# A gated hybrid decoder layer on one core: inputs laid out transposed in HBM, an opening in another order, a stacked bias table, and dilated values computed in token order

## The chip, the core and the metric

The kernel runs on one core of a Trainium2 chip. The metric is the device time of one execution in microseconds (us), the median of several runs. The engines are TensorE (PE in the rows; PEld is its loading of the stationary operand), VectorE (DVE), ScalarE (ACT), GpSimd (POOL) and SyncE (SP). SP and ACT each own a hardware DMA queue, POOL a software one.

## What is computed

One layer of a decoder over 512 tokens of width 1024, with three branches that read the same x:

```
proj = x @ w_in                       # q, k, v of 12 heads; zb; qc
A: for 3 groups (window, dilation) = (128,1), (512,4), (2048,16), 4 heads each:
     s = q k^T / 8 + bias[bucket(distance)]   # keys gathered by stride
     o = softmax(s) v                 # groups merged by their denominators
B: u, vg = split(gelu(zb));  ob = u * (tril(w_spatial) @ layer_norm(vg) + b_spatial)
C: oc = softmax(qc kc^T / 8) vc       # kc, vc = mem @ w_mem_kv, 256 memory rows
y = (sum over branches of sigmoid(x @ w_gate + b_gate) * (branch @ w_proj)) @ w_out
h = layer_norm(alpha * x + y)
out = layer_norm(alpha * h + (gelu(causal_conv3(h @ w_a)) * (h @ w_b)) @ w_ffn_down)
```

## The kernel before

All values are fp32. A large product is made of three TensorE matmuls on a type called fp32r: each operand is split into a high part (a copy to fp32r by ScalarE, `hi`) and a low part (the rest, by VectorE, `lo`), and `mm3` adds low x high, high x low and high x high. `split_of` splits an activation, `emit_split` (L133, L134) a unit of weights.

Weights stream in a fixed order. `add_load`, `cols2` and `kcols` list the loads and the units (1024 columns per partition) in each; three raw buffers hold loads, four buffers hold split units, and `unit()` takes the next one after it has split two units ahead:

```
wraw = ctx.enter_context(tc.tile_pool(name="wraw", bufs=3))
wspl = ctx.enter_context(tc.tile_pool(name="wspl", bufs=4))
AHEAD = 2
```

x must lie with its features on the partitions, since TensorE contracts over partitions. Before, x comes in token rows, and `turn_x` turns it by 32 TensorE transposes of 128x128 (tile `tx`), copies the result out of PSUM and splits it into `xTh` and `xTl`. The opening is written out by hand for TensorE, ScalarE and VectorE (`manual_schedule`): 11 matmuls on zeros (`idle`, L370), then the transposes, mixed with the first products (`first_mm`, L384) of the first two of twelve 128-column groups of q and k, each in two halves of 256 tokens (t0, t1) and two halves of the contraction. The other ten groups follow as `qk` (L220, j = 2 to 11, 24 matmuls each).

After group j = 4, `prep_small` turns a tile of small parameters (`par`), and multiplies the bias table `relb` (33 rows) with one-hot rows of the bucket of each distance (`bkt`, 33 x 384 for each head group) into `vec`. From there four transfers on POOL's queue build the biases: `vec` to HBM (`vecs`), a repeated copy (`shear`), and three skewed reads (`bias`). Behind them on the same queue comes the load of `ws`, the spatial weights, which `prep_spatial` turns by 8 transposes and masks on VectorE.

Then come the values: `v0` (two units, for dilation 1) and `v12` (four units, for the other two groups). Groups 4 and 16 read the tokens by stride 4, so the stationary operand of `v12` is read by `xr`, every fourth token of xT.

Next `zb_part` computes the gMLP's inputs while `fill()` runs pieces of attention between its matmuls. Then mem is turned by 16 transposes (`tm`), and qc, kc, vc, the gates, the output projection and the FFN follow.

Behind the opening the program's order on each engine is set by a scheduler that places instructions by its own estimate of when they are ready; each engine then executes strictly in that order.

## Time and profile before

| | |
|---|---|
| median of 3 runs | 819.17 us (818.08 to 819.25) |
| profiled execution | 819.34 us |
| its span, first to last instruction | 817.6 us |
| TensorE matmul busy | 807.9 us, 99% of the span |
| VectorE, ScalarE busy | 382.2 us, 282.6 us |
| granted TensorE clock, mean | 0.999 |

The span is what the trace covers; 1.74 us of the profiled time lie outside it. A busy TensorE says only that matmuls were in it, so the time is read from the chain of work that ended last and from the spacing of matmuls.

### The profile page before, as it was taken

What the parts mean: (1) busy time and instruction counts of PE and PEld (TensorE: products, weight loads), DVE (VectorE), ACT (ScalarE), POOL (GpSimd) and SP (SyncE); (2) the same over time, 40 slices, a digit from 0 to 9 for tenths busy, and PEclk for the clock granted to TensorE, in tenths of its full rate; (3) what the DMA queues carried; (4) which work ended last, traced back from release to release, by engine and by line L of the source; (5) the groups of instructions that cost most, each with busy time, mean ns of one, the idle gap of its engine ahead of it and who ended that gap; (6) DMA issues with size and microseconds to landing.
All of it is one profiled execution on the core that took longest, in us unless ns stands there. A gap on an engine that the chain in (4) does not pass through costs nothing.

```text
span 817.6 us, 9710 instructions
## 1 busy us (share of the span) xinstructions
PE 807.9 (99%) x4048; PEld 672.7 (82%) x4048; DVE 382.2 (47%) x591; ACT 282.6 (35%) x431; POOL 20.4 (2%) x32
## 2 busy tenths in 40 slices
PE   8999999999999999999999999999999999999996
PEld 7878997778877788888888988888888888888885
DVE  4433245835664343435857454544444445225056
ACT  4322246663365132233511243333333333224000
POOL 2001000100000000000000000000000000000000
PEclk9999999999999999999999999999999999999999
DMA  8455231123402223243840033333333323234002
GB/s 319 137 180 186 104 129 52 53 78 122 137 26 78 71 93 120 81 152 108 307 152 1 1 103 103 103 103 104 103 103 103 103 89 127 94 103 155 1 26 78
DMA packets 61772, 87.64 MB, mean 107 GB/s; under 512 B 2107, under 2 KB 49259, under 8 KB 61729
## 3 DMA queue, kind: packets, MB, share of 16 engines
q1 hardware_dynamic: 59264, 81.81, 29.6%
q0 software_dynamic: 1408, 4.17, 1.4%
q10 hardware_dynamic: 1056, 1.05, 0.4%
q8 instruction: 32, 0.52, 0.3%
q14 instruction: 12, 0.09, 0.0%
HBM read 84.89 MB, written 4.48 MB: 109 GB/s over the span
## 4 chain that ended last, share of the span: by engine, by line
PE 98%; DMA 1%; DVE 0%; issue 0%; DVEq 0%; SPq 0%
PE y L220 20%; PE gate L220 16%; PE pa L220 13%; PE pb L220 13%; PE qk L220 7%; PE zb L220 6%; PE proj L220 5%; PE v L220 4%; PE up L220 3%; PE oT L559 1%; PE qk L384 1%; PE sc L559 1%; PE qc L220 1%; PE pt L528 1%; PE vc L220 1%; PE kc L220 1%
## 5 line engine op out<-in xcount | busy, mean ns | idle before, releaser
L134 DVE TENSOR_TENSOR wl<-raw,wh 128x1024 fp32r<-128x1024 f32 (+1 forms) x128 | 153.9, 1206 | 175.3 <-ACT wh L133 165.4
L133 ACT ACTIVATE wh<-raw 128x1024 fp32r<-128x1024 f32 (+1 forms) x128 | 133.0, 1043 | 183.3 <-PE pb L220 47.2
L220 PE MATMUL y<-wh,h 128*128 128x512 f32 x256 | 79.0, 389 | 0.0
L220 PE MATMUL gate<-xTh,wl 128*128 128x512 f32 x192 | 76.7, 400 | 0.0
L220 PE MATMUL gate<-xTh,wh 128*128 128x512 f32 x192 | 75.0, 390 | 0.0
L220 PE MATMUL gate<-xTl,wh 128*128 128x512 f32 x192 | 74.9, 390 | 0.0
L220 PE MATMUL pa<-hTh,wl 128*128 128x512 f32 x160 | 62.3, 389 | 0.0
L220 PE MATMUL pa<-hTl,wh 128*128 128x512 f32 x160 | 62.3, 389 | 0.0
L220 PE MATMUL pa<-hTh,wh 128*128 128x512 f32 x160 | 62.2, 389 | 0.0
L220 PE MATMUL pb<-hTh,wl 128*128 128x512 f32 x160 | 62.2, 389 | 0.0
L220 PE MATMUL pb<-hTl,wh 128*128 128x512 f32 x160 | 62.2, 389 | 0.0
L220 PE MATMUL pb<-hTh,wh 128*128 128x512 f32 x160 | 62.2, 389 | 0.0
L220 PEld LDWEIGHTS y<-wh,h 128*128 128x128 f32 x256 | 48.0, 188 | 10.0
L220 PE MATMUL y<-wl,h 128*128 128x512 f32 x128 | 49.8, 389 | 0.0
L941 DVE SCALAR_TENSOR_TENSOR c<-pa,par,c 128x511 f32<-128x511 f32 x20 | 15.0, 751 | 65.8 <-ACT c L940 65.8
L220 PEld LDWEIGHTS gate<-xTh,wl 128*128 128x128 f32 x192 | 36.1, 188 | 8.7 <-issue 1.2
L220 PEld LDWEIGHTS gate<-xTh,wh 128*128 128x128 f32 x192 | 36.0, 188 | 7.7
L940 ACT ACTIVATE c<-pa,par 128x512 f32<-128x512 f32 x20 | 15.6, 781 | 76.1 <-PE pa L220 76.1
L220 PEld LDWEIGHTS gate<-xTl,wh 128*128 128x128 f32 x192 | 36.1, 188 | 7.0
L220 PEld LDWEIGHTS pa<-hTh,wh 128*128 128x128 f32 x160 | 30.0, 188 | 6.3
L220 PEld LDWEIGHTS pb<-hTh,wl 128*128 128x128 f32 x160 | 30.0, 188 | 6.3
L220 PEld LDWEIGHTS pa<-hTh,wl 128*128 128x128 f32 x160 | 30.1, 188 | 6.2
(223 smaller groups left out, 1485.8 us busy)
## 6 DMA issues: line engine op xcount, KB each, us to landing
raw<-in_w_ffn_up SPq DMA_DIRECT2D x22, 1024.0 KB, 4.9
raw<-in_w_in SPq DMA_DIRECT2D x13, 1024.0 KB, 5.1
raw<-in_w_gate SPq DMA_DIRECT2D x12, 1024.0 KB, 4.9
raw<-in_w_ffn_down SPq DMA_DIRECT2D x11, 1024.0 KB, 4.9
raw<-in_w_out SPq DMA_DIRECT2D x4, 1024.0 KB
shear<-vecs POOLq DMA_DIRECT2D x1, 2304.0 KB, 14.9
raw<-in_w_mem_kv SPq DMA_DIRECT2D x2, 1024.0 KB, 5.2
raw<-in_w_proj_b SPq DMA_DIRECT2D x4, 512.0 KB, 3.5
```

The lines of the kernel that those rows point to most:

```text
L133: nc.scalar.activation(h3, src, AF.Copy)
L134: nc.vector.tensor_tensor(l3, src, h3.bitcast(F32), op=ALU.subtract)
L220: nc.tensor.matmul(ps, w, v, start=first, stop=last)
L384: nc.tensor.matmul(pss[j][:, sl], w[a][:, k, :], xs(4 * kk + k, sl)[c], start=kk + k + a + c == 0, stop=kk == 1 and a == 1 and k == 3)
L528: nc.tensor.transpose(pt[:, kb, u, :], self.p[:, u, kb * P:(kb + 1) * P], ident)
L559: nc.tensor.matmul(ps, w, v, start=first, stop=last)
L940: nc.scalar.activation(c, pa, AF.Identity, bias=CB(i), scale=CW(2, i))
L941: nc.vector.scalar_tensor_tensor(c[:, 1:], pa[:, :S - 1], CW(1, i), c[:, 1:], op0=ALU.mult, op1=ALU.add)
```

## The change

The host stores five inputs in another layout: x a second time, transposed (`xt`, in four pieces of 256 tokens by 512 features), the first two column groups of w_in as contiguous pieces (`wqk0`), mem and w_spatial transposed, and all small parameters in one transposed table (`params`). The kernel drops `turn_x` and the transposes of `par`, `ws` and mem. x and the first weights are loaded in smaller pieces over SP's and ACT's queues, and the opening's matmuls come in four groups, each needing one piece of x, behind 12 idle matmuls without a break. The bias table is split into high and low rows that are stacked (97 rows), so that one fp32r matmul for each head group replaces the fp32 one. `v12` is computed before `v0`, from xT in token order, copied to HBM (`v12_d`) and read back by stride.

```
@@ -112,7 +112,11 @@
         shape, src = loads[n]
         t = wraw.tile([P, 2048], F32, tag="raw", name=f"raw{n}")
         v = t[:, :shape[1] * shape[2]].rearrange("p (a b) -> p a b", a=shape[1])
-        (nc.scalar if n < 2 else nc.sync).dma_start(v, src)
+        if n < 2:
+            for j, q in enumerate((nc.sync, nc.scalar)):
+                q.dma_start(v[:, 4 * j:4 * j + 4, :], src[j])
...
-    for k in (0, 4):
-        add_load([P, 4, 256], win[k * P:(k + 4) * P, 0:256].rearrange("(k p) c -> p k c", p=P),
-                 [lambda r: r[:, :, 0:P], lambda r: r[:, :, P:2 * P]])
+    for kk in range(2):
+        add_load([P, 8, P], wqk0[kk], [lambda r: r[:, 0:4, :], lambda r: r[:, 4:8, :]])
     for j in range(1, 6):
         cols2(win, 256 * j)
-    kcols(win, 0, 8, 1536, 256)
     for k in (0, 4):
         kcols(win, k, 4, 1792, 512)
+    kcols(win, 0, 8, 1536, 256)
...
-    for hf in range(2):
-        for b in range(2):
-            load_x(b, slice(hf * 512, hf * 512 + 512))
-        emit_load()
-    for b in (2, 3):
-        load_x(b)
+    xraw = [T8(f"x{kk}") for kk in range(2)]
+    def load_x(hf, kk, q, ks=slice(0, 4)):
+        q.dma_start(xraw[kk][:, ks, hf * 256:hf * 256 + 256], xt[hf, kk][:, ks, :])
+    def load_x2(hf, kk):
+        load_x(hf, kk, nc.sync, slice(0, 2))
+        load_x(hf, kk, nc.scalar, slice(2, 4))
+    load_x2(0, 0)
+    emit_load()
+    load_x2(1, 0)
+    load_x(0, 1, nc.sync)
+    emit_load()
+    load_x(1, 1, nc.sync)
...
-    def turn_x(b, kk):
-        ps = bank("tx")
-        for k in range(4):
-            nc.tensor.transpose(ps[:, k * P:(k + 1) * P],
-                                xraw[b // 2][:, b % 2, (kk * 4 + k) * P:(kk * 4 + k + 1) * P], ident)
-        p3 = ps.rearrange("p (k t) -> p k t", k=4)
-        split_of(xTh[kk][:, :, b * P:(b + 1) * P], xTl[kk][:, :, b * P:(b + 1) * P], p3)
+    def split_x(hf, kk):
+        sl = slice(hf * 256, hf * 256 + 256)
+        split_of(xTh[kk][:, :, sl], xTl[kk][:, :, sl], xraw[kk][:, :, sl])
...
+    relb2 = const.tile([64 + NR, 12], F32R, name="relb2")
...
-        nc.gpsimd.dma_start(rows[0:66, :], conv_w[0].rearrange("c (t p) -> (c t) p", p=P))
-        nc.gpsimd.dma_start(rows[66:88, :], conv_b[0].rearrange("(t p) -> t p", p=P))
-        nc.gpsimd.dma_start(rows[88:112, :], b_gate[0].rearrange("(t p) -> t p", p=P))
-        nc.gpsimd.dma_start(rows[112:120, :], b_spatial[0])
+        nc.vector.memset(par, 0.0)
+        nc.gpsimd.dma_start(par, params)
         nc.vector.memset(relb, 1.0)
         nc.gpsimd.dma_start(relb[0:N_BUCKETS, :], rel_bias)
-        nc.gpsimd.dma_start(bk[0:N_BUCKETS + 1], buckets)
+        nc.vector.memset(bkt[:, 0:3 * VW], 0.0)
+        for r0 in (0, 64):
+            nc.gpsimd.dma_start(bk[r0:r0 + NR], buckets)
...
-        ps = bank("par")
-        nc.tensor.transpose(ps[:, :P], rows, ident)
-        nc.vector.tensor_copy(par, ps[:, :P])
         nc.vector.tensor_scalar(gb5, par[:, 88:112], 0.5, None, op0=ALU.mult)
+        bkr = T8("bkr", F32R).rearrange("p a c -> p (a c)")[:, 0:3 * VW].rearrange("p (g c) -> p g c", g=3)
+        nc.scalar.activation(bkr, bk, AF.Copy)
+        zero = W2("zero")[:, 0:12]
+        nc.vector.memset(zero, 0.0)
+        nc.vector.tensor_copy(relb2, zero[0:64 + NR])
+        nc.vector.tensor_copy(relb2[0:NR], relb)
+        low = W2("low")[0:NR, 0:12]
+        nc.vector.tensor_tensor(low, relb, relb2[0:NR].bitcast(F32), op=ALU.subtract)
+        nc.vector.tensor_copy(relb2[64:64 + NR], low)
...
-            nc.tensor.matmul(ps[0:4, :VW], relb[:, 4 * g:4 * g + 4], bk[0:N_BUCKETS + 1, g, :],
+            nc.tensor.matmul(ps[0:4, :VW], relb2[:, 4 * g:4 * g + 4], bkr[0:64 + NR, g, :],
...
-    wsT = w4[:, 8:16, :]
+    wsT = w4[:, 0:8, :]
     def prep_spatial():
-        for hh in range(2):
-            ps = bank("wsT")
-            for g in range(4):
-                nc.tensor.transpose(ps[:, g * P:(g + 1) * P], w4[:, hh * 4 + g, :], ident)
-            nc.vector.tensor_tensor(w4[:, 8 + 4 * hh:12 + 4 * hh, :],
-                                    ps.rearrange("p (g q) -> p g q", g=4),
-                                    maskT[:, None, :].to_broadcast([P, 4, P]), op=ALU.mult)
+        nc.vector.tensor_tensor(wsT, wsT, maskT[:, None, :].to_broadcast([P, 8, P]), op=ALU.mult)
...
+    def first_group(kk, sl, order):
+        for i, (j, a, c) in enumerate(order):
+            first_mm(j, kk, sl, a, c, kk == 1 and j not in [o[0] for o in order[i + 1:]])
...
-        idle(6)
-        turn_x(0, 0)
-        turn_x(1, 0)
-        idle(5)
-        for u in range(4):
-            first_split(u)
-        first_high(0, 0, t0)
-        first_high(1, 0, t0)
-        turn_x(0, 1)
-        turn_x(1, 1)
+        idle(12)
+        ka, kb = slice(0, 2), slice(2, 4)
+        nc.scalar.activation(xTh[0][:, ka, t0], xraw[0][:, ka, t0], AF.Copy)
+        nc.vector.tensor_copy(xTh[0][:, kb, t0], xraw[0][:, kb, t0])
+        for ks in (ka, kb):
+            nc.vector.tensor_tensor(xTl[0][:, ks, t0], xraw[0][:, ks, t0], xTh[0][:, ks, t0].bitcast(F32),
+                                    op=ALU.subtract)
+        first_split(0)
+        first_split(1)
+        first_group(0, t0, ((0, 0, 0), (0, 0, 1), (1, 0, 0), (1, 0, 1), (0, 1, 0), (1, 1, 0)))
+        split_x(1, 0)
+        first_group(0, t1, ((0, 0, 0), (1, 0, 0), (0, 1, 0), (1, 1, 0), (0, 0, 1), (1, 0, 1)))
+        split_x(0, 1)
+        first_split(2)
+        first_split(3)
+        first_group(1, t0, ((0, 0, 0), (0, 0, 1), (1, 0, 0), (1, 0, 1), (0, 1, 0), (1, 1, 0)))
+        split_x(1, 1)
         load_small()
-        first_mm(0, 0, t0, 1, 0)
-        first_mm(1, 0, t0, 1, 0)
-        turn_x(2, 0)
-        first_high(0, 1, t0)
-        turn_x(3, 0)
-        first_high(1, 1, t0)
-        first_mm(0, 1, t0, 1, 0)
-        turn_x(2, 1)
-        first_mm(1, 1, t0, 1, 0)
-        turn_x(3, 1)
-        for kk in range(2):
-            for j in range(2):
-                first_high(j, kk, t1)
-            if kk == 0:
-                emit_split()
-                emit_split()
-            for j in range(2):
-                first_mm(j, kk, t1, 1, 0)
+        emit_split()
+        emit_split()
+        first_group(1, t1, ((0, 0, 0), (1, 0, 0), (0, 1, 0), (1, 1, 0), (0, 0, 1), (1, 0, 1)))
...
-            nc.gpsimd.dma_start(w4[:, 0:8, :], w_spatial[0].rearrange("g p q -> p g q"))
+            nc.gpsimd.dma_start(wsT, w_spatial)
...
+    pss = [bank(f"v12_{b}") for b in range(NB)]
+    for u in range(4):
+        w = unit()
+        for b in range(NB):
+            for k2 in range(2):
+                k = 2 * u + k2
+                mm3(pss[b], xs(k, slice(b * P, (b + 1) * P)), (w[0][:, k2, :], w[1][:, k2, :]),
+                    k == 0, k == KD - 1)
+    v12n = T8("v12n")
+    v12_d = dram.tile([S, S], F32, name="v12_d")
+    for b in range(NB):
+        nc.scalar.activation(v12n[:, b, :], pss[b], AF.Copy)
+        nc.gpsimd.dma_start(v12_d[b * P:(b + 1) * P, :], v12n[:, b, :])
+    nc.gpsimd.dma_start(v12, v12_d[:].rearrange("(l r) c -> l r c", r=4))
...
-    pss = [bank(f"v12_{r}") for r in range(4)]
-    for u in range(4):
-        w = unit()
-        for r in range(4):
-            for k2 in range(2):
-                k = 2 * u + k2
-                mm3(pss[r], xr(k, r), (w[0][:, k2, :], w[1][:, k2, :]), k == 0, k == KD - 1)
-    for r in range(4):
-        nc.scalar.activation(v12[:, r, :], pss[r], AF.Copy)
...
-    memv = memraw.rearrange("p (b a) c -> p b (a c)", b=2)
-    nc.sync.dma_start(memv, mem[0].rearrange("(b p) d -> p b d", p=P))
+    memv = memraw.rearrange("p a (b c) -> p (a b) c", b=2)
+    nc.sync.dma_start(memv, mem)
     memTh = T8("memTh", F32R)
     memTl = T8("memTl", F32R)
     mTh_, mTl_ = (t.rearrange("p a (b c) -> p (a b) c", b=2) for t in (memTh, memTl))
-    for kk in range(4):
-        ps = bank("tm")
-        p3 = ps.rearrange("p (k t) -> p k t", k=2)
-        for k in range(2):
-            for b in range(2):
-                nc.tensor.transpose(p3[:, k, b * P:(b + 1) * P],
-                                    memv[:, b, (2 * kk + k) * P:(2 * kk + k + 1) * P], ident)
-        split_of(mTh_[:, 2 * kk:2 * kk + 2, :], mTl_[:, 2 * kk:2 * kk + 2, :], p3)
+    for kk in range(2):
+        ks = slice(4 * kk, 4 * kk + 4)
+        split_of(mTh_[:, ks], mTl_[:, ks], memv[:, ks])
...
+    a["xt"] = a["x"][0].reshape(2, 256, 2, 4, P).transpose(0, 2, 4, 3, 1)
+    a["wqk0"] = a["w_in"][0][:, :256].reshape(2, 4, P, 2, P).transpose(0, 3, 2, 1, 4)
+    a["mem"] = a["mem"][0].reshape(MEM, KD, P).transpose(2, 1, 0)
+    a["w_spatial"] = a["w_spatial"][0].transpose(2, 0, 1)
+    a["params"] = np.concatenate([a["conv_w"][0].reshape(66, P), a["conv_b"][0].reshape(22, P),
+                                  a["b_gate"][0].reshape(24, P), a["b_spatial"][0]]).T
```

The places in the program's order that matter follow, each engine's instructions in order; the numbers behind names are buffer numbers. First TensorE at the start, before the change, from the last idle matmuls of the first six (`tx` is a transpose of x, `qk` a first product):

```order
L370 MATMUL idle<-still 128x512
L262 MATMUL tx<-ident,x_78 128x128 x8
L370 LDWEIGHTS still
L370 MATMUL idle<-still 128x512
...
L384 MATMUL qk_122<-xTh_104,wh_151 128x256 x4
L384 MATMUL qk_122<-xTl_106,wh_151 128x256 x4
L384 MATMUL qk_123<-xTh_104,wh_155 128x256 x4
L384 MATMUL qk_123<-xTl_106,wh_155 128x256 x4
L262 MATMUL tx<-ident,x_78 128x128 x8
L384 MATMUL qk_122<-xTh_104,wl_152 128x256 x4
L384 MATMUL qk_123<-xTh_104,wl_156 128x256 x4
L262 MATMUL tx<-ident,x_79 128x128 x4
```

The same place after the change, from the last idle matmul:

```order
L367 MATMUL idle<-still 128x512
L381 MATMUL qk_124<-xTh_106,wh_146 128x256 x4
L381 MATMUL qk_124<-xTl_108,wh_146 128x256 x4
L381 MATMUL qk_126<-xTh_106,wh_150 128x256 x4
L381 MATMUL qk_126<-xTl_108,wh_150 128x256 x4
L381 MATMUL qk_124<-xTh_106,wl_147 128x256 x4
L381 MATMUL qk_126<-xTh_106,wl_151 128x256 x4
L381 MATMUL qk_125<-xTh_106,wh_146 128x256 x4
```

The transposes are gone; the 96 first products are the same in number and shape, now grouped by piece of x.

VectorE before, at the mask of the spatial weights, behind the values of branch C:

```order
L754 COPY vcN<-vc 128x512
L134 TENSOR_TENSOR wl_1860<-raw_1857,wh_1859 128x1024
L336 TENSOR_TENSOR ws<-wsT,maskT 128x512 x2
L772 SCALAR_TENSOR_TENSOR ug<-sv,par,ug 128x4x64 x2
L134 TENSOR_TENSOR wl_1920<-raw_1857,wh_1919 128x1024
```

VectorE after, from the evacuation of `vec`; `wl_537` is the low part for group j = 11, `wl_567` that of the first `v12` unit, and each `COPY qk` evacuates one of the groups j = 8 to 11:

```order
L312 COPY vec<-vec 4x384 x3
L138 TENSOR_TENSOR wl_441<-raw_356,wh_440 128x1024
L138 TENSOR_TENSOR wl_474<-raw_356,wh_473 128x1024
L138 TENSOR_TENSOR wl_505<-raw_444,wh_504 128x1024
L228 TENSOR_TENSOR qk_122<-qk,qk_122 128x512 x2
L138 TENSOR_TENSOR wl_537<-raw_444,wh_536 128x1024
L335 TENSOR_TENSOR ws<-ws,maskT 128x1024
L360 COPY qk_120<-qk 128x512
L138 TENSOR_TENSOR wl_567<-raw_508,wh_566 128x1024
L360 COPY qk_120<-qk 128x512
L138 TENSOR_TENSOR wl_599<-raw_508,wh_598 128x1024
```

The mask no longer follows a transpose, and the scheduler has put it far earlier, ahead of the weights of `v12`; it waits there for the load of `ws`.

POOL's queue after the change, from the bias chain on:

```order
L313 DMA vecs<-vec 4x1152
L315 DMA shear<-vecs 1536x1x384
L318 DMA bias<-shear 128x4x256
L321 DMA bias<-shear 128x4x128 x2
L421 DMA ws<-in_w_spatial 128x1024
L438 DMA v_d<-v12n 128x512 x4
L440 DMA v_629<-v_d 128x2048
```

The first five kinds stand in the order of before; the last two, the way of `v12` through HBM, are new.

## Rows read from the trace of the kernel before

**Rows 1.** The page: TensorE's busy time, and the chain that ended last, by engine.

```profile
PE 807.9 (99%) x4048; PEld 672.7 (82%) x4048; DVE 382.2 (47%) x591; ACT 282.6 (35%) x431; POOL 20.4 (2%) x32
...
PE 98%; DMA 1%; DVE 0%; issue 0%; DVEq 0%; SPq 0%
```

**Rows 2.** Waits of TensorE over the span: total us, times, longest.

```profile
PE idle L370 <- DVE mhalf L254: 1.3, 1, 1.3
PE tx L262 <- DMA x<-in_x: 1.0, 2, 0.7
```

**Rows 3.** The chain in order of time, 0 to 120 us: start, us, what.

```profile
11.50 0.87 PE tx L262 x8
...
17.94 5.76 PE qk L384 x48
23.70 16.35 PE qk L220 x72
40.05 0.11 PE par L300
40.16 2.02 PE vec L307 x6
```

**Rows 4.** The chain in order of time, 100 to 320 us.

```profile
148.26 1.02 PE oT L559 x16
...
184.40 1.90 PE tm L720 x16
...
210.35 0.87 PE wsT L335 x8
```

**Rows 5.** Waits of SP's queue: total us, times, longest.

```profile
SPq L115 <- DVE wl L134: 649.2, 66, 57.2
```

**Rows 6.** Timeline, 0 to 32 us: start, us, engine, line, op, out<-in, count.

```profile
1.25 2.74 PE L370 MATMUL idle<-still 128*128 128x512 bf16 x6 [1.25 <-DVE mhalf L254]
...
7.71 1.14 ACT L133 ACTIVATE wh<-raw 128x512 fp32r<-128x512 f32 x2
...
8.75 1.32 PE L384 MATMUL qk<-xTh,wh 128*128 128x256 f32 x4
9.91 0.63 PE L384 MATMUL qk<-xTl,wh 128*128 128x256 f32 x4
```

**Rows 7.** DMA issues, 0.8 to 0.9 us: KB each, us from issue to landing.

```profile
raw<-in_w_in ACTq DMA_DIRECT2D x1, 512.0 KB, 4.5
x<-in_x SPq DMA_DIRECT2D x1, 256.0 KB, 3.3
```

**Rows 8.** DMA issues from 1.2 us: the second piece of x; landings of ACT's two loads.

```profile
x<-in_x SPq DMA_DIRECT2D x1, 256.0 KB, 4.8
DMA to landing us min/median/max: 4.5/6.4/8.2
```

**Rows 9.** Windows: us, busy us (x) of PE, PEld, DVE, ACT, POOL; PEclk, DMA share, GB/s.

```profile
7.20:8.00 0.80, 0.80 (x3) 0.30 (x2) 0.15 (x1) 0.79 (x2) 0.00 (x0) 1.00 1.10 407
91.83:114.67 22.84, 22.84 (x99) 22.80 (x98) 5.98 (x5) 6.53 (x8) 0.00 (x0) 1.00 0.33 116
```

**Rows 10.** Groups of weight loads by shape: busy us, mean ns of one, idle before.

```profile
L220 PEld LDWEIGHTS y<-wh,h 128*128 128x128 f32 x256 | 48.0, 188 | 10.0
L220 PEld LDWEIGHTS v<-wl,xTh 128*128 128x128 f32 x64 | 16.1, 251 | 0.0
```

**Rows 11.** POOL's queue, 30 to 120 us, and the landing of `ws`.

```profile
44.01 0.53 POOL L310 DMA_DIRECT2D vecs<-vec  x1 [25.31 <-DVE vec L309]
64.21 0.89 POOL L431 DMA_DIRECT2D ws<-in_w_spatial  x1
...
ws<-in_w_spatial POOLq DMA_DIRECT2D x1, 512.0 KB, 7.6
```

**Rows 12.** VectorE, 40 to 85 us.

```profile
43.18 0.54 DVE L309 COPY vec<-vec 4x384 f32<-4x384 f32 x1
...
65.29 1.23 DVE L134 TENSOR_TENSOR wl<-raw,wh 128x1024 fp32r<-128x1024 f32 x1 [0.40 <-ACT wh L133]
```

More of the change, by code (lines that the diff above doesn't have):

```diff
@@ L70, in layer_kernel @@
 def layer_kernel(
-    ctx: ExitStack, tc, x, mem, rel_bias, w_in, w_mem_kv, sg_ln_g, sg_ln_b, w_spatial, b_spatial,
-    w_proj_a, w_proj_b, w_proj_c, w_gate, b_gate, w_out, ln1_g, ln1_b, w_ffn_up, conv_w, conv_b,
+    ctx: ExitStack, tc, x, xt, wqk0, params, mem, rel_bias, w_in, w_mem_kv, sg_ln_g, sg_ln_b, w_spatial,
+    w_proj_a, w_proj_b, w_proj_c, w_gate, w_out, ln1_g, ln1_b, w_ffn_up,
     w_ffn_down, ln2_g, ln2_b, buckets, out,
@@ L227, in split_of @@
             nc.vector.scalar_tensor_tensor(lo, src, scale, hi.bitcast(F32), op0=ALU.mult, op1=ALU.subtract)
-    xraw = []
-    for h in range(2):
-        xraw.append(T8(f"x{h}").rearrange("p (b a) c -> p b (a c)", b=2))
-    def load_x(b, c=slice(0, D)):
-        nc.sync.dma_start(xraw[b // 2][:, b % 2, c], x[0][b * P:(b + 1) * P, c])
     BF16 = mybir.dt.bfloat16
@@ L352, in qk_mm, with qk_out @@
             mm3(ps[:, sl], (w[0][:, k, :], w[1][:, k, :]), xs(k, sl), k == 0, k == KD - 1)
-    def qk_out(j, ps):
+    def qk_out(j, ps, sl=slice(0, S)):
         if j % 6 < 2:
-            split_of(*qk0s(j), ps, SCALE if j < 6 else 1.0)
+            split_of(*[t[:, sl] for t in qk0s(j)], ps[:, sl], SCALE if j < 6 else 1.0)
             return
@@ L370, in idle @@
             nc.tensor.matmul(idle_ps, still[:, :P], still, start=True, stop=True)
-    pss = [bank(f"qk{j}") for j in range(2)]
     t0, t1 = slice(0, 256), slice(256, 512)
+    pss = {(j, sl.start): bank(f"qk{j}") for j in range(2) for sl in (t0, t1)}
     w2 = {}
@@ L378, in first_split, with first_mm @@
         w2[u] = prepared.pop(u)
[L380 removed]
+    def first_mm(j, kk, sl, a, c, last):
         w = w2[2 * kk + j]
         for k in range(4):
[L384 to L420 removed]
@@ new lines, in first_mm @@
+            nc.tensor.matmul(pss[j, sl.start][:, sl], w[a][:, k, :], xs(4 * kk + k, sl)[c],
+                             start=kk + k + a + c == 0, stop=last and k == 3)
+    def first_group(kk, sl, order):
+        for i, (j, a, c) in enumerate(order):
+            first_mm(j, kk, sl, a, c, kk == 1 and j not in [o[0] for o in order[i + 1:]])
+    with tc.manual_schedule(engines={mybir.EngineType.PE, mybir.EngineType.Activation, mybir.EngineType.DVE}):
+        idle(12)
[15 more added lines that the diff above has]
+        split_x(1, 1)
+        load_small()
+        emit_split()
+        emit_split()
+        first_group(1, t1, ((0, 0, 0), (1, 0, 0), (0, 1, 0), (1, 1, 0), (0, 0, 1), (1, 0, 1)))
@@ L421, in layer_kernel @@
     cursor["u"] = 4
     for j in range(2):
-        qk_out(j, pss[j])
+        for sl in (t0, t1):
+            qk_out(j, pss[j, sl.start], sl)
     for j in range(2, 12):
@@ L970, in layer_kernel, with laid_out @@
     project(NF, H2, n_wdn, lambda b: norm(H(b), lnp2, out[0][b * P:(b + 1) * P, :]))
-_INS = ['x', 'mem', 'rel_bias', 'w_in', 'w_mem_kv', 'sg_ln_g', 'sg_ln_b', 'w_spatial', 'b_spatial',
-        'w_proj_a', 'w_proj_b', 'w_proj_c', 'w_gate', 'b_gate', 'w_out', 'ln1_g', 'ln1_b',
-        'w_ffn_up', 'conv_w', 'conv_b', 'w_ffn_down', 'ln2_g', 'ln2_b']
+_INS = ['x', 'xt', 'wqk0', 'params', 'mem', 'rel_bias', 'w_in', 'w_mem_kv', 'sg_ln_g', 'sg_ln_b', 'w_spatial',
+        'w_proj_a', 'w_proj_b', 'w_proj_c', 'w_gate', 'w_out', 'ln1_g', 'ln1_b',
+        'w_ffn_up', 'w_ffn_down', 'ln2_g', 'ln2_b', 'buckets']
+def laid_out(inputs):
+    a = {n: np.asarray(v) for n, v in inputs.items()}
+    a["xt"] = a["x"][0].reshape(2, 256, 2, 4, P).transpose(0, 2, 4, 3, 1)
[4 more added lines that the diff above has]
+                                  a["b_gate"][0].reshape(24, P), a["b_spatial"][0]]).T
+    a["buckets"] = bucket_rows()
+    return a
 def kernel(**inputs):
@@ L983 @@
     arrays, args = {}, []
-    for name in _INS + ["buckets"]:
-        a = bucket_rows() if name == "buckets" else np.ascontiguousarray(inputs[name])
+    laid = laid_out(inputs)
+    for name in _INS:
+        a = np.ascontiguousarray(laid[name])
         arrays[f"in_{name}"] = a
```

19 lines of the change are left out of this document (5 added, 14 removed).

## The prediction

> **What bounds the kernel now.** I read the page first: TensorE has matmuls in it for 99% of the span, and the chain that ended last is 98% TensorE [rows 1]. A busy share alone proves little, so the next view was its waits: 2.3 us in two lines, all before 6.1 us [rows 2]. The chain in order of time then shows TensorE's work piece behind piece [rows 3, 4]. So a matmul that is taken out behind 6 us is worth its place in that chain, until a wait opens that is not there now; and the start is worth what the first product comes earlier. SP's loads wait 649.2 us for VectorE to give buffers back [rows 5]: weights are asked for when a buffer is free, and no row has TensorE wait for one.
>
> Full-rate spacings follow from counts in the chain: 48 products of 256 columns take 5.76 us, 0.120 each; 72 of 512 columns take 16.35 us, 0.227 each; eight transposes take 0.87 us, 0.109 each [rows 3].
>
> **The change part by part.** *Start.* Before, the first product starts at 8.75 us [rows 6], the first phase ends at 23.70 [rows 3], and 96 products and 24 transposes lie in between. Those transposes are 24 x 0.109 = 2.6 us and go. When can the first product start now? It needs the first quarter of x, halved over two queues, and the first weights behind it, also halved. Before, SP's first 256 KB landed 3.3 us after an issue at 0.81, at 4.1 us [rows 7]; its first 512 KB were complete at 1.20 + 4.8 = 6.0 [rows 8]; ACT's first 512 KB landed at 0.80 + 4.5 = 5.3 [rows 7]. The new bytes ahead of and including the first weights are the same 256 + 256 KB on each queue, so: x at 4.1, weights at 5.3 on ACT's queue and 6.0 on SP's. Unit 0 is on SP's. Its high part takes 1.14 / 2 = 0.57 us on ScalarE [rows 6], so the first product starts at about 6.65. ScalarE now issues four DMAs instead of two ahead of its first activation; that has to fit before x lands, and each us over costs one. Then 96 x 0.120 = 11.5 us, to 18.2 if no piece of x is late.
>
> Is one late? ACT's queue had moved 1 MB by 1.28 + 8.2 = 9.5 us [rows 8], with SP's running beside it. Group 2 needs a piece at 9.5 whose bytes are the third 256 KB on each queue (about 7.8). Groups 3 and 4 need SP's first 1.25 and 2 MB by 12.4 and 15.3; all 3.1 MB at some 400 GB/s [rows 9] from about 3 us are there by 11. I take 0.1 for small waits: the phase ends at 18.3, **5.4 us** earlier. Bounds: first product at 6.0 (ACT's landing time for both halves), gain 6.1; or the pieces late or the clock low (rivals), gain 3.2.
>
> *Clock.* The six idle matmuls take 2.74 us, 0.46 each, the 1.2 GHz level (512 columns in 0.43 us); the first four products take 1.32 us, 0.3 each instead of 0.12 [rows 6]; full spacing begins near 9.9 [rows 6], after a last wait for x, which was there at 6.0. Now 12 idle matmuls run unbroken from 1.25, 5.2 us at the low level, and the products follow within a few tenths of a us. I take full rate from the first product on.
>
> *Small parameters and bias table.* `par` and six passes of `vec` hold the chain for 40.05 to 42.18, 2.13 us [rows 3]. No row has an fp32r matmul of 384 columns; three of them lie between 3 x 0.120 and 3 x 0.227, 0.36 to 0.68; I take 0.52, between the neighbours. **1.6 us**. ScalarE's copy of the one-hot table (1152 columns, about 1.2) and the tiny VectorE steps are ready near 26 us, the matmul is due at 18.3 + 16.35 = 34.6: without that cover of 8 us each us late costs one.
>
> *v12.* Its 96 products take 22.84 us [rows 9], 0.238 each against 0.227. The group of weight loads says why: a load of strided x takes 251 ns, others 188 [rows 10]. In token order 96 x 0.227 = 21.8: **1.0 us**, between 0 and 1.1. The Trainium skill, SBUF — State Buffer, section Door 1: The DMA port swizzle, says that accesses which leave a 16-byte line pay, and yet that four fp32 elements can be stepped over for free. Four fp32 is exactly this stride; by the second half this term would be 0 and the sum 9.7. The trace bears out the first half: it is not free here.
>
> The way through HBM costs nothing if it is back in time: `v12` ends near 95 us, 96 with its copies; four stores like the load of `ws` (7.6 to land, 0.9 to issue [rows 11]) and a 1 MB read of at most twice that make 120. The first dilated product before was at 148.26, 33.6 us behind the end of the values [rows 4, 9]; now 95 + 11.5 (`v0`, 96 products of 0.120) + 33.6 = 140. Cover 20 us.
>
> *mem and w_spatial.* 16 transposes hold the chain for 1.90 us, 8 for 0.87 [rows 4]. Less a little for the seam, **1.8 and 0.9 us**. mem's splits on ScalarE and VectorE keep their sum of columns.
>
> *The moved mask.* VectorE now reaches the mask behind `wl_537`, and it must wait there for `ws`, which stands last in the bias chain on POOL's queue. From the first `vecs` issue to the landing of `ws` it takes 64.21 + 7.6 - 44.01 = 27.8 us [rows 11]. The `vec` matmul starts at 34.6, three copies of 0.54 follow [rows 12], the chain starts near 36.8 and `ws` is there at 64.6. `wl_537` ends near 53, so VectorE stands still for some 11 us. Queued behind it: the evacuations of groups 8 to 11 and the low parts for `v12`. The first of these is ready at 64.6 + 1.2 + 0.7 + 1.23 [rows 12] = 67.7; TensorE wants it at 34.6 + 0.5 + 7 x 5.45 = 73.2 (5.45 a group, from 16.35 for three). So a new wait, but 5.5 us of cover: price 0, beyond it 1 us per us.
>
> **Sum.** 5.4 + 1.6 + 1.0 + 1.8 + 0.9 = 10.7 us off the profiled execution's 819.34 us (which stands 0.17 above the median): **808.6 us**, span 806.9. Bounds of the terms: 6.1 + 1.8 + 1.1 + 1.9 + 0.9 = 11.8 (807.5) and 3.2 + 1.4 + 0 + 1.7 + 0.8 = 7.1 (812.2).
>
> **The rivals.** *A: the clock is low at the first products.* TensorE falls idle between the last idle matmul (5.7 to 6.4 us) and the first product. For: before, full spacing came 3.9 us after the last wait (6.0 to 9.9). Against: the pause here is under 1 us, and nothing shows a fall. If it takes that long again, 13 products at 0.3 replace 32 at 0.12: 2.3 us lost, 810.9.
>
> *B: the pieces of x land late.* For: SP's queue carries 2 MB of the 3, and at the pace of ACT's second half-megabyte (9.5 - 5.3 = 4.2 us per 512 KB [rows 7, 8]) its 1.5 MB for the second weights would be there at 13.6, not 11, and group 3 would start near 14.2 instead of 12.4: 1.8 us, 810.4. Against: ACT's queue is done by 9.5 and leaves SP the rest. The Trainium skill, DMA: Bandwidth & Descriptors, section Issuing engines are not separate DMA queues, speaks for B: a second issuing engine saves issue time only, since all share 16 DMA engines. The 407 GB/s with both queues at work [rows 9] does not contradict it.
>
> *C, the other side: VectorE's wait for `ws` reaches TensorE.* For: in-order VectorE, a chain of five transfers, the load last. It decides from a chain 5.5 us longer on, and from 16.2 us (44 instead of 27.8) the kernel is slower than before; twice the chain (55.6) would give 808.6 + 22.3 = 830.9. Against: the same transfers took 27.8 beside the same loads.
>
> *D: the gain is given back.* Earlier TensorE would run into weights that are not yet there, near 818. Against: SP waits for buffers, not for data [rows 5].
>
> **How the numbers follow.** Forecast 0.66, A 0.12, B 0.15, C 0.03 (about half of it slower than before), D 0.03, and 0.01 for what is not named. The time is the forecast's, 808.6. The range takes in its bounds and A and B, with the runs' own scatter below: 807.2 to 812.0. Changes within 0.2% (1.6 us) are about what a measurement of this kernel cannot tell from none. Faster 0.95, same 0.03, slower 0.02.
>
> **What would show it.** The first product at 6.5 to 6.8 us with 0.12 spacing at once, and the first phase over near 18.3; spacing of 0.3 speaks for A, waits of TensorE for ScalarE or VectorE between 12 and 16 us for B. `vec` at 34 to 35 us for about 0.5; weight loads of `v12` at 188 ns; no `tm`, no `wsT`. A VectorE wait of 8 to 14 us ahead of the mask, with none of TensorE behind it; if TensorE waits for `wl` near 73 us, C holds. I am wrong if the chain shows a DMA or VectorE behind 20 us, or if the first phase ends later than 20.5.

## The result and the profile after

| | before | changed |
|---|---|---|
| median (runs) | 818.78 us (818.08 to 819.25, 4 runs) | 809.97 us (809.41 to 810.34, 4 runs) |
| ratio | | 0.989, 95% interval 0.9878 to 0.9902 |
| profiled execution, its span | 819.34, 817.6 | 810.0, 808.1 |

The kernel is 1.1% faster: 8.8 us by the medians, 9.34 by the two profiled executions. 808.6 was forecast, in a range of 807.2 to 812.0. The changed kernel run again beside later experiments took 810.06 us (809.33 to 810.85, 4 runs), ratio 0.9895 (0.988 to 0.991).

The page after, beside [rows 1]: TensorE has 9.9 us less in it, but the chain that ended last is 96% TensorE, not 98; DMA has 2% of it instead of 1, and VectorE 1% instead of 0.

```profile
PE 798.0 (99%) x3989; PEld 660.9 (82%) x3989; DVE 382.0 (47%) x592; ACT 282.7 (35%) x428; POOL 21.7 (3%) x35
...
PE 96%; DMA 2%; DVE 1%; SPq 0%; issue 0%; ACT 0%; ACTq 0%; DVEq 0%
```

TensorE's waits after, beside [rows 2] (total us, times, longest). Three are new, and one of them, at `gate`, is far behind the start: that is the thing to follow.

```profile
PE idle L367 <- DVE zero L300: 1.3, 1, 1.3
PE qk L381 <- ACT xTh L226: 0.5, 1, 0.5
PE gate L223 <- DVE wl L138: 0.2, 1, 0.2
PE qk L381 <- ACT wh L137: 0.2, 1, 0.2
```

The timeline of TensorE's start, beside [rows 6]. The first product stands at 6.04 us instead of 8.75, and at full rate; the second group waits for a piece of x.

```profile
1.26 4.58 PE L367 MATMUL idle<-still 128*128 128x512 bf16 x12 [1.26 <-DVE zero L300]
6.04 0.74 PE L381 MATMUL qk<-xTh,wh 128*128 128x256 f32 x4 [0.20 <-ACT wh L137]
6.62 0.64 PE L381 MATMUL qk<-xTl,wh 128*128 128x256 f32 x4
...
9.65 1.22 PE L381 MATMUL qk<-xTh,wh 128*128 128x256 f32 x8 [0.48 <-ACT xTh L226]
...
18.38 0.40 PE L223 MATMUL qk<-xTh,wl 128*128 128x512 f32 x1
```

Where the time came from is read by laying the same landmarks of the two timelines side by side: the start of the first record of each phase on TensorE.

| first record of | before | after | earlier by | new since the line above |
|---|---|---|---|---|
| the 72 products behind the first phase | 23.53 | 18.38 | 5.15 | 5.15, the opening |
| `vec` | 40.09 | 34.73 | 5.36 | 0.21, `par` gone |
| the 168 products behind `vec` | 42.11 | 35.25 | 6.86 | 1.50, `vec` |
| `v` | 80.32 | 73.35 | 6.97 | 0.11 |
| `zb` | 114.50 | 106.62 | 7.88 | 0.91, the values |
| `qc` | 186.06 | 176.43 | 9.63 | 1.75, mem's transposes |
| `gate` | 208.79 | 199.61 | 9.18 | -0.45, the wait |
| last `y` record | 809.77 | 799.83 | 9.94 | 0.76, `wsT` less gaps in the first gate |
| end of the profiled execution | 819.34 | 810.0 | 9.34 | -0.60, behind the last product |

So everything that the change takes off TensorE arrived, and about 1.2 us went at two places that the prediction did not name: 0.56 at the gate and 0.60 behind the last product. The chain after, in order of time, leaves TensorE between `lse` and `gate` (start, us, what):

```profile
180.82 0.23 PE lse L606 x2
...
186.74 1.38 DMA wgt_d<-lt
188.14 0.66 SPq L623
...
188.85 4.58 DMA wide<-wgt_d
...
193.53 0.76 DVE wide L631 x2
...
195.16 0.59 DVE wide L632
195.75 1.03 DVE wl L138
196.81 0.68 DVE wide L632
197.49 0.60 DVE oaT L228
198.09 0.34 DVE kcT L228
198.43 1.14 DVE wl L138
...
199.61 2.56 PE gate L223 x10
```

The weights for merging the two attention parts go out to HBM and come back as `wide`. VectorE stands in order behind that read; the low half of the first gate's weights, `wl`, is queued behind the merge, and TensorE waits for `wl`. Before, the same chain ran, and the last `wl` ended in time, at 208.4:

```profile
202.36 1.29 DVE L635 TENSOR_TENSOR wide<-wide,oA 128x512 f32<-128x512 f32 x2 [2.08 <-DMA wide<-wgt_d]
...
207.18 1.22 DVE L134 TENSOR_TENSOR wl<-raw,wh 128x1024 fp32r<-128x1024 f32 x1
...
208.79 0.40 PE L220 MATMUL gate<-xTh,wl 128*128 128x512 f32 x1
```

The moved mask, on VectorE: it waits 9.96 us for `ws` and starts at 64.55; the work behind it catches up before `v` starts at 73.35.

```profile
64.55 1.23 DVE L335 TENSOR_TENSOR ws<-ws,maskT 128x1024 f32<-128x1024 f32 x1 [9.96 <-DMA ws<-in_w_spatial]
...
66.30 1.22 DVE L138 TENSOR_TENSOR wl<-raw,wh 128x1024 fp32r<-128x1024 f32 x1
```

The weight loads of `v` by shape, beside [rows 10]: mean 190 ns, not 251.

```profile
L223 PEld LDWEIGHTS v<-wl,xTh 128*128 128x128 f32 x64 | 12.1, 190 | 1.3
```

### The profile page after: what moved, and what is told of

It is laid out like the page before. It is cut to its first block, busy times and chain, and to the rows that moved or that the text cites. A ratio compares the mean times of both kernels' runs of the same rounds, so it can differ in the third digit from the quotient of the medians.

```text
span 808.1 us, 9605 instructions
## 1 busy us (share of the span) xinstructions
PE 798.0 (99%) x3989; PEld 660.9 (82%) x3989; DVE 382.0 (47%) x592; ACT 282.7 (35%) x428; POOL 21.7 (3%) x35
## 4 chain that ended last, share of the span: by engine, by line
PE 96%; DMA 2%; DVE 1%; SPq 0%; issue 0%; ACT 0%; ACTq 0%; DVEq 0%
PE y L223 20%; PE gate L223 16%; PE pa L223 13%; PE pb L223 13%; PE qk L223 7%; PE zb L223 6%; PE proj L223 5%; PE v L223 4%; PE up L223 3%; PE oT L555 1%; PE sc L555 1%; PE pt L524 1%; PE qk L381 1%; DMA x<-in_xt 1%; DMA wide<-wgt_d 1%; PE qc L223 1%
## 5 line engine op out<-in xcount | busy, mean ns | idle before, releaser
L223 PEld LDWEIGHTS pb<-hTl,wh 128*128 128x128 f32 x160 | 30.0, 188 | 6.3
L223 PEld LDWEIGHTS pb<-hTh,wh 128*128 128x128 f32 x160 | 30.1, 188 | 6.3
```

The source lines that it names most:

```text
L223: nc.tensor.matmul(ps, w, v, start=first, stop=last)
```

## The experiments

Every kernel computes the whole layer; one leaves out warm-up products. The effects are tenths of a microsecond to two, at the edge of what the times tell, so each is judged by where its TensorE phases start in its own trace, and the times stand beside it. Landmarks are those of the table above.

**Parts undone one at a time.** First the bias vectors in full fp32:

```diff
-            nc.tensor.matmul(ps[0:4, :VW], relb2[:, 4 * g:4 * g + 4], bkr[0:64 + NR, g, :],
+            nc.tensor.matmul(ps[0:4, :VW], relb[:, 4 * g:4 * g + 4], bk[0:NR, g, :],
```

> The changed kernel with one part undone: the three products for the bias vectors are again in full fp32 from the unstacked table (before: 2.02 us for six records, rows 3, against 0.52 us now). Theory: these products stand on TensorE's own path with nothing to hide them, so the products behind them start 1.5 us later, and the whole is 1.5 us longer, 811.5. Rival (a part of it is given back behind, as with mem): the first gate product and the end come later by 1.0 us only, since the wait of 0.2 us and the gaps at the gate are then covered (the chain that makes the gate wait starts from TensorE's transposes, and moves along with TensorE): on the theory the gate's wait stays.

812.32 us (811.82 to 812.61), ratio 0.9919 (0.9905 to 0.9934). TensorE's timeline:

```profile
34.38 2.10 PE L310 MATMUL vec<-bkt,relb 33*4 33x384 f32 x6
36.41 0.50 PE L223 MATMUL qk<-xTh,wl 128*128 128x512 f32 x1
...
74.62 0.39 PE L223 MATMUL v<-wh,xTl 128*128 128x512 f32 x1
...
201.19 0.50 PE L223 MATMUL gate<-xTh,wl 128*128 128x512 f32 x1 [0.55 <-DVE wl L138]
```

From `vec` to the next product 2.03 us instead of 0.52: 1.51, nothing given back. From there to `v` 38.21 instead of 38.10, which accounts for the 0.11 of the table. The wait at `gate` is larger here, 0.55, and not gone.

The dilated values with every fourth token as weights (`xr` takes them from the split x), straight into `v12`:

```diff
-                mm3(pss[b], xs(k, slice(b * P, (b + 1) * P)), (w[0][:, k2, :], w[1][:, k2, :]),
+                mm3(pss[b], xr(k, b), (w[0][:, k2, :], w[1][:, k2, :]),
...
-        nc.scalar.activation(v12n[:, b, :], pss[b], AF.Copy)
-        nc.gpsimd.dma_start(v12_d[b * P:(b + 1) * P, :], v12n[:, b, :])
-
-    nc.gpsimd.dma_start(v12, v12_d[:].rearrange("(l r) c -> l r c", r=4))
+        nc.scalar.activation(v12[:, b, :], pss[b], AF.Copy)
```

> The changed kernel with one part undone: the dilated values are again computed with every fourth token as weights (strided weight loads) and need no way through HBM; the order of the column blocks stays that of the change. Theory: the strided weight loads (251 ns against 188 ns, rows 10) are what cost 0.91 us of this block before: v takes 34.2 us instead of 33.27, all that is behind starts 0.9 us later. Rival (the 0.9 us came from the order of v0 and v12, or the way through HBM disturbs something later): the block stays at 33.3 us, or the loss is given back by 140 us, where the first value products read v12.

811.07 us (810.08 to 812.12), ratio 0.9905 (0.989 to 0.992). `v` starts at 72.81 and `zb` at 106.88: 34.07 us instead of 33.27, so 0.80 of the 0.91 come from the strided loads. Its weight loads by shape:

```profile
L223 PEld LDWEIGHTS v<-wl,xTh 128*128 128x128 f32 x64 | 16.0, 251 | 0.0
```

The page of the Trainium skill that the prediction weighed here (SBUF — State Buffer, section Door 1: The DMA port swizzle) lets a stride of four fp32 elements pass for free; the same loads at 251 and 190 ns decide against that for TensorE's weight loads. TensorE did not wait for the way through HBM: `v12` was back at 100.48 + 8.4 = 108.9 us and first used at 140.32. But that way was not free. The time outside the span (device time less span) is 1.67 to 1.86 us in 21 runs of the kernel before, 1.86 to 2.47 in 46 runs of all the kernels with the way through HBM, and 1.68 to 1.72 in the four runs of this one, without it. By the medians (1.72 and 2.05) it gives back about 0.3 of the 0.91; what takes that time, no trace shows.

The spatial weights as they come, with the eight transposes in the gate phase:

```diff
+        for hh in range(2):
+            ps = bank("wsT")
+            for g in range(4):
+                nc.tensor.transpose(ps[:, g * P:(g + 1) * P], w4[:, hh * 4 + g, :], ident)
...
-            nc.gpsimd.dma_start(wsT, w_spatial)
+            nc.gpsimd.dma_start(w4[:, 0:8, :], w_spatial[0].rearrange("g p q -> p g q"))
```

> The changed kernel with one part undone: the spatial weights come as they are, and 8 TensorE transposes (0.87 us, rows 4) and the mask from their output bank stand in the gate phase again. Theory: nothing hides them, TensorE's work behind them comes 0.9 us later, and VectorE no longer waits at 54 to 65 us, which changes nothing before. Rival (a part of the gap at the first gate product takes them up): the whole comes 0.4 us later or less.

810.78 us (810.69 to 811.03), ratio 0.9904 (0.9888 to 0.9921). From the first gate product (199.53) to the last `y` record (800.60) it takes 601.07 us; the changed kernel takes 600.22 and, run again, 600.21. That is the forecast 0.9, and nothing takes it up.

mem in token rows, with its 16 transposes:

```diff
+    for kk in range(4):
+        ps = bank("tm")
...
+                nc.tensor.transpose(p3[:, k, b * P:(b + 1) * P],
+                                    memv[:, b, (2 * kk + k) * P:(2 * kk + k + 1) * P], ident)
+        split_of(mTh_[:, 2 * kk:2 * kk + 2, :], mTl_[:, 2 * kk:2 * kk + 2, :], p3)
```

> The changed kernel with one part undone: mem comes in token rows again and is transposed by 16 TensorE transposes (1.90 us before, rows 4). Theory: their removal gave 1.9 us at its place, but the merge weights' chain of DMAs behind it does not move with TensorE, so that about 0.5 us of it was lost again as a wait for wl ahead of the first gate product (199.61 us; 9.80 us earlier than before at qc, 9.35 us at gate). With the transposes back, qc starts about 1.9 us later, the wait of the first gate product for wl (0.2 us, and gaps of about 0.24 us inside its first 12 products) is gone, and the first gate product starts at about 201.0 to 201.2: the whole is longer than the changed kernel by about 1.3 us. Rival (the 0.45 us lost at the gate has nothing to do with mem): the gate's wait stays, and the whole is longer by 1.9 us.

811.09 us (810.91 to 811.97), ratio 0.9904 (0.9888 to 0.9921). `zb` to `qc` takes 71.53 us instead of 69.81, so the transposes were worth 1.72. And the wait at the gate is gone, as my theory had it:

```profile
178.24 0.48 PE L223 MATMUL qc<-xTh,wl 128*128 128x512 f32 x1
...
201.03 0.50 PE L223 MATMUL gate<-xTh,wl 128*128 128x512 f32 x1
```

The numbers fit and the theory is nevertheless wrong. `lse`, which starts the chain of the merge, stands 4.2 us *behind* `qc` in both kernels (4.19 before, 4.23 after), so transposes ahead of `qc` move the chain and the gate alike and cannot cover it. The run with one warm-up product, which keeps mem as changed, has no wait at the gate either. The runs taken together show what decides.

**What makes TensorE wait at the gate.** For every profile but two that follow, from its timeline: us from SP's issue of the `wide` read to VectorE's first use of it, us from `lse` to that use, and us from the first `qc` product to the first `gate` product. The last column has the start of the nearest fetch of 16 KB of instructions, in us from the issue of the read; what it means follows.

| kernel | `wide` read | `lse` to use | `qc` to `gate` | fetch |
|---|---|---|---|---|
| before | 4.72 | 12.11 | 22.73 | -8.83 |
| one idle product (below) | 4.88 | 12.34 | 22.78 | 3.63 |
| mem turned | 5.07 | 12.52 | 22.79 | -2.27 |
| `ws` first (below) | 5.24 | 12.69 | 23.00 | 1.02 |
| changed, again | 5.28 | 12.72 | 23.04 | 1.06 |
| changed | 5.39 | 12.87 | 23.18 | 1.01 |
| `ws` turned | 5.59 | 13.05 | 23.36 | 1.01 |
| `ws` slowed (below) | 5.68 | 13.14 | 23.47 | 1.01 |
| `vec` fp32 | 5.70 | 13.16 | 23.49 | 0.61 |
| `ws` slowed more (below) | 5.72 | 13.17 | 23.50 | 1.14 |
| `v12` strided | 5.86 | 13.33 | 23.65 | 1.28 |
| loads exchanged (below) | 5.94 | 13.40 | 23.72 | 1.55 |

From 12.69 down the table the fourth column is the one before it plus 10.31 to 10.33; above it stands at 22.7 to 22.8, TensorE's own work. So the wait is the length of one read, 512 KB fetched out of 8 KB in HBM, beyond some 5.0 us; the profile before had 0.3 us to spare.

What lengthens the read goes with the last column. Queue q8 carries fetches of instructions, 16 KB each, 31 of them in the changed kernel for 3989 matmuls and as many weight loads: one for about 257 TensorE instructions. A change that takes TensorE instructions out moves all later fetches. DMA queues (packets, MB, share of 16 engines) around the read, first before the change (196 to 200.5 us), then after it (186 to 191 us):

```profile
q1 hardware_dynamic: 228, 0.38, 27.7%
```

```profile
q1 hardware_dynamic: 210, 0.34, 22.2%
q8 instruction: 1, 0.02, 1.2%
```

Where the fetch starts ahead of the read or while its last packets start (3.63 us), the read takes 4.72 to 5.07 us and TensorE does not wait, in three profiles of three. Where it starts 0.61 to 1.55 us into the read, the read takes 5.24 to 5.94, in nine of nine here, and 5.49 and 5.52 in the two that follow. So, as far as fourteen profiles show it, the change did lengthen the read: with fewer TensorE instructions ahead, a fetch fell into it. The transposes of mem moved the fetch out again, and so did leaving out eleven warm-up products, 180 us earlier. No run moves a fetch alone, and why it costs the read that much, and what spreads the rest, stays open.

Two kernels take VectorE's work out from between the read and `wl`. The first lets the merge wait five more steps of the side work:

```diff
-        for _ in range(4):
+        for _ in range(9):
             yield
```

> The changed kernel with the merge of the two attention parts given up 5 steps later in the code that feeds the scheduler, so that two of its VectorE operations (oaT, 0.68 us each) stand behind the first gate's weight halves instead of ahead of them. Theory: the first gate product waited for wl (0.2 us, and gaps of 0.24 us in its first 12 products), since wl stood on VectorE behind operations that wait for the merge weights' chain of DMAs; with 0.68 us less ahead of it the wait goes: the first gate product starts at 199.4, and the end comes 0.4 us earlier. Rival (the gaps come from something else): the gate's first 12 products take 3.02 us as before.

810.04 us (809.97 to 810.68), ratio 0.9889 (0.9874 to 0.9904). The read took 5.52, yet `qc` to `gate` is 22.77: the wait is gone, more than the expected 0.4. But from `gate` to the last `y` record it takes 600.87 us instead of 600.22: all side steps behind move by some products, and what was won is lost there; at which step, I did not follow. The second keeps the steps and moves two splits only, to the step that follows mem's products:

```diff
-            split_of(oaT[:, hp, :], oaT[:, 2 + hp, :], wt)
+            merged.append(wt)
             yield
...
         prep_spatial()
+        for hp in range(2):
+            split_of(oaT[:, hp, :], oaT[:, 2 + hp, :], merged[hp])
+        ready.add("a")
```

> The changed kernel with the splits of the two merged attention rows (on ScalarE and VectorE, 0.63 and 0.68 us each) given up later in the code, at the step that follows the key and value products of mem, so that they stand behind the first gate's weights; the order of TensorE's work stays word for word. Theory: the wait ahead of the first gate product is VectorE's, not TensorE's own order; with 0.68 to 1.36 us less ahead of the first gate's wl, the first gate product starts 22.8 us after the first qc product in every execution (23.2 in the changed kernel, up to 23.7 in others), and what follows takes as long as before (600.1 to 600.2 us to the last product): 0.4 to 0.9 us faster than the changed kernel. Rival one: the gap stays at 23.2 or more, since wl waits for something else. Rival two: the gap goes and is given back behind, as in the run with five later steps, where the products behind the gate's start took 0.65 us longer.

809.22 us (808.96 to 809.45), ratio 0.9885 (0.987 to 0.9899), beside the changed kernel's 810.06 on the same chip. VectorE in that stretch, where both halves of `wl` now stand ahead of `oaT`:

```profile
193.18 1.29 DVE L631 TENSOR_TENSOR wide<-wide,oA 128x512 f32<-128x512 f32 x2 [2.90 <-DMA wide<-wgt_d]
...
197.06 0.42 DVE L228 TENSOR_TENSOR kcT<-kc,kcT 128x256 fp32r<-128x256 f32 x1
197.39 2.53 DVE L138 TENSOR_TENSOR wl<-raw,wh 128x1024 fp32r<-128x1024 f32 x2
```

TensorE goes on without a gap:

```profile
198.66 0.28 PE L223 MATMUL vc<-wh,memTh 128*128 128x256 f32 x1
198.78 0.40 PE L223 MATMUL gate<-xTh,wl 128*128 128x512 f32 x1
```

With a read of 5.49 us, `qc` to `gate` is 22.78 and `gate` to the last `y` 600.11: 0.36 less than the changed kernel beside it (23.04 + 600.21), 0.51 less than the one profiled first. That the wait comes from VectorE's order behind the read is shown by that. The median is lower by 0.84; the two intervals overlap, so the times alone do not settle the gain.

**The opening.** Eleven warm-up products left out:

```diff
-        idle(12)
+        idle(1)
```

> The changed kernel with 1 warm-up product on TensorE instead of 12, so that TensorE has done next to nothing when its first real products come at 6.04 us. Theory: what TensorE did before decides the clock of these products, and the 12 idle products cover them in full: with one, the first group's products run at half the rate (about 0.24 us each for 256 columns instead of 0.12) for some 4 us of work, and the first phase ends 1.5 to 3 us later than 18.55. Rival (the clock is at its full level whatever came before): the phase ends at 18.55 and the time is the same.

812.19 us (811.31 to 813.53), ratio 0.992 (0.9905 to 0.9935). TensorE's timeline:

```profile
6.18 1.22 PE L381 MATMUL qk<-xTh,wh 128*128 128x256 f32 x4 [4.31 <-ACT wh L137]
7.20 1.05 PE L381 MATMUL qk<-xTl,wh 128*128 128x256 f32 x4
8.05 1.05 PE L381 MATMUL qk<-xTh,wh 128*128 128x256 f32 x4
...
13.74 1.12 PE L381 MATMUL qk<-xTl,wh 128*128 128x256 f32 x8
...
20.46 0.40 PE L223 MATMUL qk<-xTh,wl 128*128 128x512 f32 x1
```

A product of 256 columns takes 0.21 us at first (four from 7.20 to 8.05), where the changed kernel takes 0.12, and 0.12 from 13 us on; the first phase ends 2.08 us later. So products with nothing ahead of them do run at half rate, the 1.2 GHz level by their spacing, and the idle products are worth 2.08 us, 2.65 against the changed kernel run again. That is near rival A's price of 2.3, but not its mechanism: there a pause of under 1 us behind the idle products was to bring the low level on. In the profiles with twelve idle products TensorE waited up to 1.01 us ahead of the first product, and the products behind took 0.12 each all the same (the first four 0.15).

Two loads exchanged on SP's queue:

```diff
-    load_x(0, 1, nc.sync)
     emit_load()
+    load_x(0, 1, nc.sync)
     load_x(1, 1, nc.sync)
```

> The changed kernel with two loads of the opening exchanged on SP's queue: the second weights' half (256 KB) ahead of the third x piece (512 KB). Theory: TensorE waited 0.48 us at 9.65 us because the x piece of its second group landed at 8.45 us, sharing the DMA engines with the third x piece issued right behind it; with 256 KB less beside it that piece lands about 0.4 to 0.6 us earlier, the wait goes, and the first phase ends about 0.4 us earlier than 18.55. Rival (that piece's landing is set by something other than what is queued behind it): no change at 9.65. A third way: the third x piece, now issued later (about 4.3 us), lands after 10.3 us and TensorE waits for it at 12.62: no gain or a loss.

810.54 us (810.02 to 811.02), ratio 0.9893 (0.9878 to 0.9908). Inconclusive. The piece landed by 8.12 us, but in nine other executions with the loads in the changed kernel's order the split of that piece began at 7.5 to 7.8 and TensorE did not wait for it either; with 8.5 in the changed kernel and a like wait in mem turned, the exchange lies inside the scatter. Over all ten profiles with those loads and twelve idle products the first phase ended between 17.81 and 18.47.

**VectorE's wait for `ws`.** The load ahead of everything on POOL's queue:

```diff
+        nc.gpsimd.dma_start(wsT, w_spatial)
         nc.vector.memset(par, 0.0)
...
-            nc.gpsimd.dma_start(wsT, w_spatial)
```

> The changed kernel with the load of the spatial weights issued ahead of everything else on POOL's queue, so that VectorE's mask never waits for it (9.96 us of waiting, until 64.55 us, in the changed kernel). Theory: that wait was hidden by about 5.5 us of slack, so its removal changes nothing: TensorE's phases start where they did, the time is that of the changed kernel within 0.2 us. Rival (VectorE's wait does cost TensorE something): the block of v starts or ends earlier, by the amount that it cost.

811.32 us (810.65 to 813.54), ratio 0.9907 (0.9891 to 0.9924). Without the wait nothing moves behind the opening: from the 72 products to `v` 54.97 us in both kernels, and `v` takes 33.27 in both. What it did move was the opening, where 512 KB more are under way; the split of the second piece of x, on ScalarE:

```profile
9.31 1.06 ACT L226 ACTIVATE xTh<-x 128x1024 fp32r<-128x1024 f32 x1 [2.55 <-DMA x<-in_xt]
```

The first phase ended at 19.16, outside the bounds of those ten, and the expected equal time did not come: the median is 1.3 above the changed kernel's. Then the load made slower, 32 columns of 1024 in single elements (`ws_flat` and `wsp_flat` are the tile and its source with the 1024 columns on one axis):

```diff
-            nc.gpsimd.dma_start(wsT, w_spatial)
+            nc.gpsimd.dma_start(ws_flat[:, 0:992], wsp_flat[:, 0:992])
+            for e in range(2):
+                cut = lambda v: v[:, 992:1024].rearrange("p (a b) -> p a b", b=2)[:, :, e:e + 1]
+                nc.gpsimd.dma_start(cut(ws_flat), cut(wsp_flat))
```

> The changed kernel with the spatial weights' load made slower: the last 32 of its 1024 columns are read in two transfers with single elements as pieces, while the mask keeps its place in VectorE's order. It measures the cover of VectorE's wait. Theory: TensorE waits by what the mask is late beyond about 5.5 us after 64.55 us: a mask at 70 us costs nothing, a mask at 75 us makes the products of v wait for wl about 5 us. Rival one (the cover is far less, since the other work queued behind the mask on VectorE is wanted earlier): a wait of TensorE that begins with a mask at 66 or 67 us. Rival two (VectorE's order does not matter to TensorE here): no wait at any delay.

810.2 us (809.78 to 810.35), ratio 0.989 (0.9873 to 0.9906). The mask came at 67.36 and TensorE had no wait at `v`. With 128 columns so:

> As the run with a slowed load of the spatial weights, with 128 of the 1024 columns instead of 32 in single elements, so that the mask comes later still (in that run it came at 67.4 us, 2.8 us later than in the changed kernel, and TensorE did not wait). Theory: the cover is about 5.5 us; wl for the first products of v is ready about 3 us after the mask's start (67.36 and 70.3 there) and wanted when v starts, at 72.9 to 73.5: with the mask at M, v starts at about M + 3.1 if that is later than 73. Rival: no wait at any delay.

829.64 us (829.12 and 830.15), ratio 1.0134 (1.0114 to 1.0154). On VectorE:

```profile
87.56 1.23 DVE L335 TENSOR_TENSOR ws<-ws,maskT 128x1024 f32<-128x1024 f32 x1 [33.35 <-DMA ws<-in_w_spatial]
...
89.30 1.22 DVE L138 TENSOR_TENSOR wl<-raw,wh 128x1024 fp32r<-128x1024 f32 x1
```

TensorE's waits:

```profile
PE v L223 <- DVE wl L138: 17.2, 1, 17.2
```

The mask stands 23.0 us later than in the changed kernel and TensorE waits 17.2: the cover is 5.8 us, or 6.2 when the two openings, 0.4 us apart, are laid over each other; 5.5 was forecast. Windows of that kernel (busy us of PE, PEld, DVE, ACT, POOL; PEclk, DMA share, GB/s) show a second price:

```profile
90.50:96.00 5.50, 5.43 (x13) 4.27 (x14) 5.22 (x7) 0.00 (x0) 0.00 (x0) 0.50 0.46 140
96.00:101.00 5.00, 5.00 (x23) 4.14 (x22) 1.18 (x1) 1.06 (x1) 0.00 (x0) 0.98 0.79 266
```

Behind the wait the granted clock is 0.50, the 1.2 GHz level, and products of 512 columns take 0.43 us instead of 0.23 for over 5 us. From `v` to `zb` it takes 53.39 us, 20.1 more than the 33.27 of the changed kernel.

## Why the prediction was right, and where it was off

The sign, the range and the mechanism held; the sum of 10.7 was 1.4 too large against 9.34, and 1.9 against the 8.8 of the medians. That the time stayed in the range is in part luck: its upper part was made for rivals A and B, of which little came, and the 1.2 us that were lost instead were in no rival. The prediction's own sign of being wrong, a DMA or VectorE in the chain behind 20 us, did come, at 186.74 to 199.61. By its own terms:

- *Opening*, 5.4: 5.15 by the profile, 5.72 when run again (17.81). Of the 0.25 that lack, 0.17 come from counting from 23.70, a time of the chain, where the timeline has the same record at 23.53. Beyond that two misses cancelled: the first weights were there by 5.4 us, where I had 6.0 on SP's queue, so the first product came 0.6 earlier; the second group's wait for x cost 0.7 in that execution (12.34 us from the first product to the end of the phase, 11.60 when run again). Rival B holds for that wait in two profiles of ten, not for 1.8 at group 3. Rival A did not come: the clock did not fall in the pause behind the idle products.
- *Small parameters and bias table*, 1.6: 1.71, with 0.11 more behind it. `vec` took the 0.52 that I chose between the bounds.
- *v12*, 1.0: 0.91; 0.80 of it by the undoing. That its way through HBM "costs nothing if it is back in time" was wrong by about 0.3 us outside the span.
- *mem*, 1.8: 1.75. *w_spatial*, 0.9: 0.86 by the undoing.
- *The moved mask*, price 0 with a cover of 5.5 us: right, the mask at 64.55 where 64.6 stood, the cover 5.8 to 6.2 measured. Rival C has the mechanism and its point of decision, and the kernel is 5.8 us from it; its price of 1 us per us leaves out the clock, which made 20.1 us out of 17.2.
- *What failed* is the step "a matmul that is taken out behind 6 us is worth its place in that chain, until a wait opens that is not there now", of which I looked for one wait only, the mask's. I did not go through the other waits of VectorE that were nearly late: the merge's read back from HBM had 0.3 us to spare, the change laid a fetch of instructions into it, and it cost 0.56 (0.45 at the gate's start, and 0.11 in its first products). Rival D named a gain given back, but by weights not yet there; the weights were there, their low half was not.
- The remaining 0.60 lie behind the last product, 0.4 to the end of the span and 0.2 outside it. The start of the last `y` record stands 7.84 us ahead of the span's end before, 8.24 to 8.25 in all thirteen profiles with the change. The last store lands 6.94 us behind that record before, and 6.97 to 6.98 after; behind its landing come 0.90 us before, and 1.26 to 1.27 after. The traces' records of semaphores (no view lists them) show why: SyncE closes the program with ten waits in a row, 0.06 us each. The last store's semaphore is in the tenth of them before and in the fourth after, so six more waits follow its landing. The 0.2 outside the span goes with the way of `v12` through HBM, as its undoing shows.

## What to carry to other kernels

When work on the bounding engine is taken out, list every place where another engine, standing in order behind a transfer, delivers with less than a microsecond to spare; a fixed trip to HBM whose length scatters by that much becomes a wait, and moving a few operations that nobody needs yet from behind the transfer to later is enough to close it. To shift side work by whole steps closes the same wait and can lose as much elsewhere, so compare the stretch behind too. And one profile that agrees with an "undone" experiment shows little if the quantity scatters: lay all the executions side by side first, and look for what else the edit moved: here it moved the fetches of instructions.
